# Two heads on the partitions of the sample-token search, whole f32 blocks beside one scatter, and a common budget for two background queues

## The chip, the cores and the metric

The kernel runs on one core of one Trainium2 chip. The metric is the device time of one execution in microseconds (us), lower is better. The profile is one profiled execution of the same program.

## The reference, cut to what matters

One inference step of a two-layer decoder trunk, for 256 prompt tokens and 8 x 8 = 64 sample tokens that share the weights. A layer has a mixing part (retention and a gated recurrence) and then PEER, a retrieval over 128 x 128 single-neuron experts with 8 heads and the 16 best per head:

```
def peer(xn, wq, keys, u_tab, v_tab):
    q = (xf @ wq).reshape(n, PEER_HEADS, 2, PEER_DKEY // 2)
    s = jnp.einsum('nhpd,hpkd->nhpk', q, keys)
    top_s, top_i = lax.top_k(s, PEER_TOPK)
    cand = top_s[:, :, 0, :, None] + top_s[:, :, 1, None, :]
    best_s, best_c = lax.top_k(cand.reshape(n, PEER_HEADS, PEER_TOPK * PEER_TOPK), PEER_TOPK)
    ...
    eidx = (i1 * N_KEYS + i2).reshape(n, PEER_HEADS * PEER_TOPK)
    gate = jax.nn.softmax(best_s, axis=-1)
    ...
        u = jnp.take(u_tab, eb, axis=0)
        hid = jax.nn.gelu(jnp.einsum('nd,nkd->nk', xb, u)) * gb
        v = jnp.take(v_tab, eb, axis=0)
        return jnp.einsum('nk,nkd->nd', hid, v)
```

Each token thus finds the 16 best of 128 keys in each of two halves for each head (the search), the 16 best of their sums (the choice), and takes the weighted rows of 128 experts.

## The kernel before, in words

**Items.** The program is a list of items, one per weight block of 128 x 1024 f32 (512 KB): a layer has 96 blocks of dense weights, the last 16 of them the key projection (wq), and then 256 blocks of the expert tables. `run` walks over the items. For item k it splits block k + 2, issues the load of block k + 5 (`RAWS`) on SP's queue, runs the item's matmuls, and then what was put off to it (`late`, filled by `at`) and the item's `post`. To split (L211) is to make two halves of a block that TensorE can take in one pass: `hi`, a rounded copy by ScalarE (L218), and `lo`, the rest, by VectorE (L220; for most wq blocks by GpSimd). Three matmuls (hi hi, lo hi, hi lo) then stand for one of full width. `hi` and `lo` have three buffers each, the loaded blocks (`raw`) five.

**PEER for the prompt tokens is dense.** All experts are computed for all 256 prompt tokens: phases of 32 blocks each, in the order U1, U0, U3, V1, U2, V0, V3, V2. A U block (`umm`, L917 to L919) has 24 matmuls of 256 columns and makes the hidden values h of 128 experts. A V block (`vmm`, L1125 to L1127) has 12 matmuls of 512 columns; they add h times the block to four accumulators, and h is split too, two blocks ahead (`hsplit`: hh by ScalarE, hl by VectorE, L1108). Between U and V h is multiplied by the gates. Those come by `scatter` (L1038): for each of 32 groups of 8 tokens VectorE builds one-hot tiles sA, sO and sB (L1054 to L1058), TensorE multiplies them (`place`, 16 small matmuls, L1068 and L1069) and VectorE multiplies h with the outcome (L1075); the group g is built in one step, placed in the next and weighed in the one after, so 34 steps in all. The scatter of U1 and U0 runs in U3, that of U3 and U2 in V0.

**Search and choice.** For each of the 16 wq blocks (8 heads, 2 halves) `post_wq` computes the scores one item later and the search one item after that: `top16` (L874), five VectorE operations with three loads of match values, for three token tiles: two of 128 prompt tokens and one of 64 sample tokens. `choose(t)` (L932) makes of them the choice per token tile: a top16 per head over 50 sums, then comparisons and sums over 2048 elements (L966, L974, L978) for the indices. It runs for tile 2 (the sample tokens), 0 and 1.

**The sample tokens are sparse.** `sample` (L1160) gathers for 64 columns one row of the U table per partition (`gather`, an indirect DMA that GpSimd issues, 512 KB, three buffers) and multiplies it with the tokens (L1180), a gather two steps ahead; then the same with the V table (L1192, L1194). The partitions hold the 64 tokens twice, each half with the experts of four heads.

**Two background queues.** `choose` and `scatter` are generators in a queue `bg`, `sample` is one in `bg2`. Twice per item `background` steps them: each queue has a credit, to which half of the item's budget is added, and each step takes off what it yields, a nominal cost in us (a scatter step 2.3, a step of `sample` 1.3). The budgets are written out by phase (`TUNE`, `bg` and `bg2`). At the start of U3 the choosers are drained, at the start of a V phase the scatter that it needs, and three blocks before the end of V2 all that is left.

All engines work off their own instructions in the program's order, so the order in which these generators are stepped is the order on VectorE.

Of the kernel before, what the change touches and what calls it, by code (L numbers as in the profile page):

```python
# [58 lines left out]
def share(i, f):  # L59
    return "pool" if math.floor((i + 1) * f) > math.floor(i * f) else "dve"  # L60


class Background:
# [28 lines left out]
class Trunk:  # L92
# [130 lines left out]
    def run(self):  # L223
        self.items, self.blocks, self.raw, self.hl = [], [], {}, {}
        for l in range(self.depth):
            Layer(self, l).plan()
        self.credit = self.credit2 = 0.0
# [37 lines left out]
class Layer:  # L265
# [5 lines left out]
    def plan(self):  # L271
# [3 lines left out]
        def add(mm, post=None, pre=None, lo="dve", budget=2.0, budget2=0.0):  # L275
            T.items.append(dict(mm=mm, post=post, pre=pre, lo=lo, budget=budget, budget2=budget2))
# [30 lines left out]
        for ph, (kind, q) in enumerate(PHASES):  # L307
            for i in range(PHB):
                e = q * PHB + i
                pre = (lambda kind=kind, q=q: self.phase(kind, q)) if i == 0 else None  # L310
                mm, post = (self.umm, self.post_u) if kind == "U" else (self.vmm, self.post_v2)
                add(mm(q, i), lambda post=post, q=q, i=i: post(q, i), pre=pre, lo=share(i, TUNE["lo"][ph]),
                    budget=TUNE["bg"][ph], budget2=TUNE["bg2"][ph])
                T.blocks.append(a["ut"][e] if kind == "U" else a["peer_v"].rearrange("(p j) d -> j p d", j=KEYS)[e])
# [617 lines left out]
    def choose(self, t):  # L932
        T, nc, pp = self.T, self.nc, self.pp
        n = TOK[t][1]
        m = lambda tag, *x, **k: self.part(("s_" if t == 2 else "p_") + tag, *x, **k)
        vals, idx = self.vals[t], self.idx[t]
        ixh = m("c_ixh", [128, 2 * HEADS, TOPK], F16)
        nc.vector.tensor_copy(ixh[:n], idx[:n].rearrange("p h s k -> p (h s) k"))
        step = m("c_step", [128, 2 * HEADS, TOPK, 2], F16)
        nc.vector.tensor_copy(step[:n, :, 0, :], ixh[:n, :, 0, None].to_broadcast([n, 2 * HEADS, 2]))  # L940
        nc.vector.tensor_tensor(step[:n, :, 1:, :], ixh[:n, :, 1:, None].to_broadcast([n, 2 * HEADS, TOPK - 1, 2]),
                                ixh[:n, :, :TOPK - 1, None].to_broadcast([n, 2 * HEADS, TOPK - 1, 2]), op=OP.subtract)
        yield 0.8
        cand = m("c_cand", [128, HEADS, NCAND])
        off = 0
        for r in range(8):
            w = ROWS[r]
            nc.vector.tensor_tensor(cand[:n, :, off:off + w], vals[:n, :, 0, r:r + 1].to_broadcast([n, HEADS, w]),
                                    vals[:n, :, 1, 0:w], op=OP.add)
            off += w  # L950
        nc.vector.tensor_tensor(cand[:n, :, off:], vals[:n, :, 0, 8:16],
                                vals[:n, :, 1, 0:1].to_broadcast([n, HEADS, 8]), op=OP.add)
        yield 1.2
        best = m("c_best", [128, HEADS, TOPK])
        pos = m("c_pos", [128, HEADS, TOPK], U32)
# [32 lines left out]
        start = m("c_start", [128, HEADS * half, 2], F16)  # L988
# [14 lines left out]
        nc.vector.tensor_tensor(g[:n], g[:n], z[:n, :, None].to_broadcast([n, HEADS, TOPK]), op=OP.mult)  # L1003
# [93 lines left out]

    def hsplit(self, q, i, upto=NPT):
# [11 lines left out]

    def vmm(self, q, i):
        nc, T = self.nc, self.T

        def mm(hi, lo):
            if i + 2 < PHB:
                self.hsplit(q, i + 2)
            else:
                self.look_ahead("V", q, i)
# [146 lines left out]
def prepare(inp, depth):  # L1265
# [11 lines left out]
    for l in range(depth):  # L1277
# [8 lines left out]
        wall[l, 80:96] = fm(i["peer_wq"][l])  # L1286
# [66 lines left out]
```

## Time and profile before

| | |
|---|---|
| median of 3 runs | 2598.59 us (2595.16 to 2600.17) |
| the profiled execution's own time | 2597.29 us |
| its span, first to last instruction | 2595.5 us |
| mean granted TensorE clock | 0.987 |
| TensorE matmul busy | 2429.8 us (94%) |
| VectorE busy | 2060.9 us (79%) |
| ScalarE busy | 1125.4 us (43%) |
| GpSimd busy | 481.1 us (19%) |
| HBM over the span | 203 GB/s |

Busy is the time in which an engine has at least one instruction in work. The durations of instructions that follow one another overlap in the record, on TensorE by much and on VectorE by a little, so a sum of durations is more than the busy time, and the pace is read from the starts. The engine names in the rows are PE (TensorE matmul), PEld (its weight load), DVE (VectorE), ACT (ScalarE), POOL (GpSimd) and SP (the queue that issues the loads). The two layers run alike; windows are given for the first. There the end of wq lies before 471.6 us, and the phases from there are U1 (to 597.8), U0 (to 690.3), U3 (to 817), V1 (to 905.2), U2 (to 997.3), V0 (to 1123), V3 (to 1212.5) and V2 (to 1300).

### The profile page before, as it was taken

The numbers are of one execution on the slowest core, as the hardware profiler recorded it, in microseconds if no ns is written. First come the engines' busy times: TensorE is split into PE (matmuls) and PEld (weight loads), VectorE is DVE, ScalarE is ACT, GpSimd is POOL, SyncE is SP. The second block draws the span as 40 slices with busy tenths as digits, with TensorE's granted clock in tenths as the row PEclk, the third lists the DMA queues.
The fourth block names the chain that finished last, engine by engine and source line by source line (L and its number), as shares of the span: only waits on it lengthen the run. The fifth ranks groups of instructions, "written<-read, shape, count | busy, mean of one in ns | idle before, by whom it ended". The sixth has DMA issues, their size and how long they took to land. (4 is left out here: it accounts for less than half of the span.)

```text
span 2595.5 us, 43089 instructions
## 1 busy us (share of the span) xinstructions
PE 2429.8 (94%) x16636; PEld 2189.7 (84%) x16636; DVE 2060.9 (79%) x3915; ACT 1125.4 (43%) x1687; POOL 481.1 (19%) x305
## 2 busy tenths in 40 slices
PE   8999999889989999899999999998899899998998
PEld 7879888889988898678888799897799888976787
DVE  6465658997799868999874756589978998699997
ACT  4337344344433444344543463443443344433444
POOL 0000004002212421035200000050021233210452
PEclk9999999999999999999999999999999999999999
DMA  6333443347767986579852334343487679865896
GB/s 235 105 110 118 135 152 120 119 162 248 263 200 237 327 292 228 170 262 350 287 192 94 114 122 148 122 145 118 154 278 249 202 257 329 290 204 164 293 353 216
DMA packets 151469, 529.73 MB, mean 204 GB/s; under 512 B 18272, under 2 KB 25440, under 8 KB 150496
## 3 DMA queue, kind: packets, MB, share of 16 engines
q1 hardware_dynamic: 112528, 385.59, 45.2%
q0 software_dynamic: 36864, 134.23, 14.2%
q10 hardware_dynamic: 1872, 7.16, 0.7%
q8 instruction: 130, 2.13, 0.3%
q14 instruction: 75, 0.61, 0.1%
HBM read 520.59 MB, written 6.32 MB: 203 GB/s over the span
## 5 line engine op out<-in xcount | busy, mean ns | idle before, releaser
L220 DVE TENSOR_TENSOR lo<-raw,hi 128x1024 fp32r<-128x1024 f32 x680 | 828.4, 1220 | 315.5 <-ACT hi L218 311.9
L218 ACT CAST hi<-raw 128x1024 fp32r<-128x1024 f32 x704 | 737.5, 1048 | 668.9 <-PE ps_acc L1127 405.6
L919 PE MATMUL ps_h<-xh,lo 128*128 128x256 f32 x2048 | 587.6, 287 | 46.5 <-DVE lo L220 46.4
L917 PE MATMUL ps_h<-xh,hi 128*128 128x256 f32 x2048 | 588.7, 287 | 0.0
L918 PE MATMUL ps_h<-xl,hi 128*128 128x256 f32 x2048 | 582.6, 284 | 0.0
L919 PEld LDWEIGHTS ps_h<-xh,lo 128*128 128x128 f32 x2048 | 396.2, 193 | 55.0 <-DVE lo L220 54.9
L1125 PE MATMUL ps_acc<-hi,hh 128*128 128x512 f32 x1024 | 405.2, 396 | 5.3 <-ACT hh L1107 5.3
L1127 PE MATMUL ps_acc<-hi,hl 128*128 128x512 f32 x1024 | 399.1, 390 | 0.0
L1126 PE MATMUL ps_acc<-lo,hh 128*128 128x512 f32 x1024 | 398.7, 389 | 0.0
L917 PEld LDWEIGHTS ps_h<-xh,hi 128*128 128x128 f32 x2048 | 396.3, 193 | 0.8 <-issue 0.7
L918 PEld LDWEIGHTS ps_h<-xl,hi 128*128 128x128 f32 x2048 | 396.4, 194 | 0.1
L1171 POOL DMA_INDIRECT g<-in_peer_u,eS x128 | 194.8, 1522 | 728.9 <-DVE g L1180 442.8
L349 PE MATMUL ps_acc<-xh,hi 128*128 128x320 f32 x960 | 309.9, 323 | 3.0 <-ACT hi L218 3.0
L351 PE MATMUL ps_acc<-xh,lo 128*128 128x320 f32 x960 | 300.8, 313 | 8.4 <-DVE lo L220 8.4
L350 PE MATMUL ps_acc<-xl,hi 128*128 128x320 f32 x960 | 299.4, 312 | 0.0
L1171 POOL DMA_INDIRECT g<-in_peer_v,eS x128 | 206.8, 1616 | 484.9 <-DVE xs L1194 424.7
L1125 PEld LDWEIGHTS ps_acc<-hi,hh 128*128 128x128 f32 x1024 | 192.3, 188 | 44.8 <-ACT hh L1107 7.0
L1127 PEld LDWEIGHTS ps_acc<-hi,hl 128*128 128x128 f32 x1024 | 192.2, 188 | 40.7
L1126 PEld LDWEIGHTS ps_acc<-lo,hh 128*128 128x128 f32 x1024 | 192.5, 188 | 38.0
L927 ACT ACTIVATE H<-ps_h 128x512 f32<-128x512 f32 x128 | 76.5, 597 | 293.2 <-PE ps_h L919 290.6
L349 PEld LDWEIGHTS ps_acc<-xh,hi 128*128 128x128 f32 x960 | 183.2, 191 | 15.0 <-issue 6.6
L351 PEld LDWEIGHTS ps_acc<-xh,lo 128*128 128x128 f32 x960 | 182.9, 191 | 11.2 <-DVE lo L220 11.0
(277 smaller groups left out, 3480.2 us busy)
## 6 DMA issues: line engine op xcount, KB each, us to landing
raw<-in_ut SPq DMA_DIRECT2D x256, 512.0 KB
raw<-in_peer_v SPq DMA_DIRECT2D x256, 512.0 KB
raw<-in_wall SPq DMA_DIRECT2D x192, 512.0 KB
r<-in_r0t SPq DMA_DIRECT2D x2, 2048.0 KB
out_sr_s<-r ACTq DMA_DIRECT2D x2, 2048.0 KB
aux<-in_c_mP SPq DMA_DIRECT2D x16, 192.0 KB
gw<-in_gates SPq DMA_DIRECT2D x2, 1024.0 KB
H<-in_keyst SPq DMA_DIRECT2D x32, 64.0 KB
```

Source lines behind the costliest of these rows:

```text
L218: nc.scalar.copy(hi, raw)
L220: eng.tensor_tensor(lo, raw, hi.bitcast(F32), op=OP.subtract)
L349: nc.tensor.matmul(o, wh, xh[:, k, :], start=k == 0, stop=False)
L350: nc.tensor.matmul(o, wh, xl[:, k, :], start=False, stop=False)
L351: nc.tensor.matmul(o, wl, xh[:, k, :], start=False, stop=k == 7)
L917: nc.tensor.matmul(o, uh, xh, start=k == 0, stop=False, skip_group_check=True)
L918: nc.tensor.matmul(o, uh, xl, start=False, stop=False, skip_group_check=True)
L919: nc.tensor.matmul(o, ul, xh, start=False, stop=k == 7, skip_group_check=True)
L1125: nc.tensor.matmul(self.acc[t][d], hh[:, s], hi[:, c], start=first, stop=False)
L1126: nc.tensor.matmul(self.acc[t][d], hh[:, s], lo[:, c], start=False, stop=False)
L1127: nc.tensor.matmul(self.acc[t][d], hl[:, s], hi[:, c], start=False, stop=last)
L1171: nc.gpsimd.indirect_dma_start(out=g, out_offset=None, in_=T.a[tab].rearrange("l e d -> (l e) d"), in_offset=bass.IndirectOffsetOnAxis(ap= ...
```

## The change

1. **Search.** The wq blocks are reordered (in the host's layout of the weights, as the two heads are then neighbours) so that heads h and h + 4 follow each other. The queries of the 64 sample tokens of both stand side by side, and their scores fill the two halves of the partitions of one tile, which one top16 searches. Prompt tokens are searched per head as before. The key slots go from 6 to 4, the queries' from 3 of 320 to 2 of 640 columns.
2. **Choice.** `choose(2)` works on 128 partitions and 4 heads in place of 64 and 8; the indices and gates come out as `sample` wants them. The yields of its top16 change from 0.7 to 1.2 (1.25 for the prompt tiles).
3. **Whole blocks.** In V0, the blocks 2, 4, 7, 9, 12, 14, 17, 19, 22, 24, 27 and 29 are not split, nor is their h: four f32 matmuls of 512 columns take both as they are. The load that reuses the slot is issued after these matmuls. The option to make `lo` on GpSimd by share (`share`, all zeros) goes.
4. **One budget.** One credit and one budget per phase: the first queue is stepped, and what it leaves goes to the second.

```
-            bg=(1.9, 1.4, 2.3, 0, 0.1, 2.3, 0.5, 0.1),
-            bg2=(0.1, 0.7, 0.7, 0.9, 0.9, 0.3, 1.1, 0.9),
-            lo=(0, 0, 0, 0, 0, 0, 0, 0))
+            peer=(1.45, 1.6, 2.5, 1.1, 1.66, 2.6, 1.1, 1.2))
...
     def split(self, k):
...
+        if self.items[k]["whole"]:
+            self.hl[k] = (raw, None)
+            return
...
             self.split(k + 2)
-            self.load(k + RAWS)
+            if not it["whole"]:
+                self.load(k + RAWS)
             for _ in it["mm"](*self.hl.pop(k)):
                 self.background(it, 0.5)
+            if it["whole"]:
+                self.load(k + RAWS)
...
     def background(self, it, f):
-        self.credit = min(self.bg.advance(self.credit + f * it["budget"]), 0.0)
-        self.credit2 = min(self.bg2.advance(self.credit2 + f * it["budget2"]), 0.0)
+        left = self.bg2.advance(self.bg.advance(self.credit + f * it["budget"]))
+        self.credit = min(left, 0.0)
...
-    def post_wq(self, c):
+    def post_wq(self, n):
-        h, s = c // 2, c % 2
-        q = self.slot("q", NT, 3)
-        nc.scalar.copy(q, self.p[:, :NT])
-        key = self.slot("key", KEYS, 6)
-        nc.sync.dma_start(key, a["keyst"][:, c, :])
+        h, s, second = n // 4 + n % 2 * 4, n // 2 % 2, n % 2
+        if not second:
+            self.q2 = self.slot("q", 2 * NT, 2)
+        q2 = self.q2
+        if second:
+            nc.scalar.copy(q2[:, NT:NT + NST], self.p[:, NPT:NT])
+            nc.scalar.copy(q2[:, NT + NST:], self.p[:, :NPT])
+            q = q2[:, NT + NST:]
+        else:
+            nc.scalar.copy(q2[:, :NT], self.p[:, :NT])
+            q = q2[:, :NPT]
+        key = self.slot("key", KEYS, 4)
+        nc.sync.dma_start(key, a["keyst"][:, 2 * h + s, :])
...
-            for t, (r0, n) in enumerate(TOK):
-                nc.tensor.matmul(p[:n, t * 128:(t + 1) * 128], q[:, r0:r0 + n], key, start=t == 0, stop=True,
+            for t in range(2):
+                nc.tensor.matmul(p[:, t * 128:(t + 1) * 128], q[:, t * 128:(t + 1) * 128], key, start=t == 0, stop=True,
                                  skip_group_check=True)
+            if second:
+                for t, k in ((2, first_key), (3, key)):
+                    nc.tensor.matmul(p[:, t * 128:(t + 1) * 128], q2[:, NPT:NPT + 2 * NST], k, start=False, stop=True,
+                                     skip_group_check=True)
             nc.scalar.copy(sc[:, 0:2, :], p[:, :256].rearrange("p (t k) -> p t k", t=2))
-            nc.scalar.copy(sc[:64, 2, :], p[:64, 256:384])
+            if second:
+                nc.scalar.copy(sc[:64, 2, :], p[:64, 256:384])
+                nc.scalar.copy(sc[64:, 2, :], p[64:, 384:512])
...
-                for t, (_, n) in enumerate(TOK):
-                    self.top16(self.slot("mr", KEYS, 3)[:n], self.vals[t][:n, h, s, :], self.idx[t][:n, h, s, :], sc[:n, t, :])
+                for t in range(3 if second else 2):
+                    hh = h if t < 2 else h - 4
+                    self.top16(self.slot("mr", KEYS, 3), self.vals[t][:, hh, s, :], self.idx[t][:, hh, s, :], sc[:, t, :])
...
     def choose(self, t):
-        n = TOK[t][1]
+        n, nh = 128, (4 if t == 2 else HEADS)
...
-        for h in range(HEADS):
+        for h in range(nh):
             self.top16(m("c_mr", [128, NCAND], bufs=2)[:n], best[:n, h, :], pos[:n, h, :], cand[:n, h, :])
-            yield 0.7
+            yield 1.2 if t == 2 else 1.25
...
-            for s in range(2):
-                nc.vector.tensor_copy(self.eS[s * 64:(s + 1) * 64], ei[:n, s * 64:(s + 1) * 64])
-                nc.vector.tensor_copy(self.gS[s * 64:(s + 1) * 64], gf[:n, s * 64:(s + 1) * 64])
+            nc.vector.tensor_copy(self.gS, gf)
+            nc.vector.tensor_copy(self.eS, ei)
...
+    def whole(self, kind, q, i):
+        return (kind, q) == ("V", 0) and i > 1 and i % 5 in (2, 4)
+
     def vmm(self, q, i):
+        def direct(w, _):
+            self.hsplit_next(q, i)
+            for t in range(2):
+                for d in range(2):
+                    nc.tensor.matmul(self.acc[t][d], self.h[q][:, i, t * 128:(t + 1) * 128], w[:, d * 512:(d + 1) * 512],
+                                     start=False, stop=False)
+                if t == 0:
+                    yield
+
+        if self.whole("V", q, i):
+            return direct
...
-        wall[l, 80:96] = fm(i["peer_wq"][l])
+        wall[l, 80:96] = fm(i["peer_wq"][l])[[2 * (n // 4 + n % 2 * 4) + n // 2 % 2 for n in range(16)]]
```

`hsplit_next` is the splitting of h two blocks ahead that stood in `mm`, left out where that block is whole. In the rest of `choose` the number of heads, nh, stands in place of `HEADS`.

## Rows read from the trace of the kernel before

**Rows 1.** The page of the profile, its head.
```profile
span 2595.5 us, 43089 instructions
```

**Rows 2.** Stretches: window, length, busy us by engine (instructions), clock, DMA share, GB/s.
```profile
450.00:471.60 21.60, 21.60 (x146) 20.14 (x144) 20.27 (x106) 8.37 (x18) 7.17 (x3) 1.00 0.33 108
471.60:597.80 126.20, 101.65 (x779) 97.10 (x779) 117.65 (x419) 49.20 (x62) 3.06 (x2) 0.97 0.45 145
597.80:690.30 92.50, 92.50 (x774) 92.50 (x773) 64.48 (x81) 44.55 (x54) 24.76 (x18) 1.00 0.83 279
690.30:817.00 126.70, 112.68 (x1281) 108.78 (x1281) 125.02 (x193) 42.31 (x51) 25.28 (x18) 1.00 0.64 206
...
905.20:997.30 92.10, 92.10 (x769) 92.10 (x768) 61.77 (x63) 41.53 (x50) 24.65 (x20) 1.00 0.87 299
997.30:1123.00 125.70, 111.32 (x896) 84.72 (x896) 124.61 (x197) 43.62 (x65) 10.90 (x8) 1.00 0.53 171
1123.00:1212.50 89.50, 87.57 (x394) 72.18 (x390) 82.66 (x96) 43.85 (x66) 47.01 (x27) 1.00 0.93 330
1212.50:1300.00 87.50, 87.22 (x386) 71.93 (x384) 73.78 (x87) 45.50 (x69) 26.82 (x16) 1.00 0.82 293
```

**Rows 3.** VectorE's timeline, searches in the first blocks of U1: start, us.
```profile
472.26 0.28 DVE L876 MAX8 H<-H 128x8 f32<-128x128 f32 x1
...
473.84 0.27 DVE L876 MAX8 H<-H 64x8 f32<-64x128 f32 x1
...
475.38 1.20 DVE L220 TENSOR_TENSOR lo<-raw,hi 128x1024 fp32r<-128x1024 f32 x1
...
492.80 2.33 DVE L220 TENSOR_TENSOR lo<-raw,hi 128x1024 fp32r<-128x1024 f32 x2
```

**Rows 4.** Timeline of VectorE and TensorE, one block of V0.
```profile
1043.19 1.21 DVE L220 TENSOR_TENSOR lo<-raw,hi 128x1024 fp32r<-128x1024 f32 x1
...
1043.33 0.20 PE L1068 MATMUL ps_m<-sB,sA 128*128 128x64 f16 x1 [0.24 <-DVE H L1075]
...
1043.82 0.48 PE L1125 MATMUL ps_acc<-hi,hh 128*128 128x512 f32 x1
...
1044.32 0.42 DVE L1108 TENSOR_TENSOR hl<-H,hh 128x256 fp32r<-128x256 f32 x1
...
1044.65 0.68 DVE L1054 TENSOR_TENSOR sA<-i1T,iota_a 128x1024 f16<-128x1024 f16 x1
...
1046.92 1.21 DVE L220 TENSOR_TENSOR lo<-raw,hi 128x1024 fp32r<-128x1024 f32 x1
```

**Rows 5.** The choice in U1: a group of VectorE's lines, and its timeline.
```profile
L974 DVE TENSOR_TENSOR steps<-H 128x2048 f16<-128x2048 f16 (+1 forms) x8 | 9.7, 1217 | 0.1
...
498.21 0.20 DVE L876 MAX8 H<-H 64x8 f32<-64x50 f32 x1
...
499.36 0.18 DVE L876 MAX8 H<-H 64x8 f32<-64x50 f32 x1
```

**Rows 6.** TensorE by source line (ns min/median/max), and its timeline (start, us).
```profile
L1125 PE MATMUL ps_acc<-hi,hh x1024: 389/389/506, 817.0 to 2585.7; 128*128 128x512 f32 x171
...
L721 PEld LDWEIGHTS ps_m<-xc,gw x64: 187/190/338, 191.4 to 1509.2; 128*128 128x128 f32 x64
L721 PE MATMUL ps_m<-xc,gw x64: 452/452/939, 191.4 to 1509.5; 128*128 128x344 f32 x64
...
200.22 1.32 PE L721 MATMUL ps_m<-xc,gw 128*128 128x344 f32 x4
```

**Rows 7.** DMA issues by line: count, median us to landing; in U0, V0, V3.
```profile
g<-in_peer_u,eS POOLq DMA_INDIRECT x18, 6.4
...
g<-in_peer_v,eS POOLq DMA_INDIRECT x8, 5.2
...
g<-in_peer_v,eS POOLq DMA_INDIRECT x27, 7.6
```

**Rows 8.** A stretch of 30 us in V3, columns as in rows 2.
```profile
1180.00:1210.00 30.00, 30.00 (x134) 24.83 (x133) 27.17 (x32) 14.96 (x23) 16.41 (x10) 1.00 0.98 362
```

More of the change, by code (lines that the diff above doesn't have):

```diff
@@ L226, in run @@
             Layer(self, l).plan()
-        self.credit = self.credit2 = 0.0
+        self.credit = 0.0
         for k, it in enumerate(self.items):
@@ L273, in plan, with add @@
         n0 = len(T.items)
-        def add(mm, post=None, pre=None, lo="dve", budget=2.0, budget2=0.0):
-            T.items.append(dict(mm=mm, post=post, pre=pre, lo=lo, budget=budget, budget2=budget2))
+        def add(mm, post=None, pre=None, lo="dve", budget=2.0, whole=False):
+            T.items.append(dict(mm=mm, post=post, pre=pre, lo=lo, budget=budget, whole=whole))
         x = lambda: (T.xh, T.xl)
@@ L311, in plan @@
                 mm, post = (self.umm, self.post_u) if kind == "U" else (self.vmm, self.post_v2)
-                add(mm(q, i), lambda post=post, q=q, i=i: post(q, i), pre=pre, lo=share(i, TUNE["lo"][ph]),
-                    budget=TUNE["bg"][ph], budget2=TUNE["bg2"][ph])
+                add(mm(q, i), lambda post=post, q=q, i=i: post(q, i), pre=pre, budget=TUNE["peer"][ph],
+                    whole=self.whole(kind, q, i))
                 T.blocks.append(a["ut"][e] if kind == "U" else a["peer_v"].rearrange("(p j) d -> j p d", j=KEYS)[e])
@@ L849, in part @@
         return v
-    def post_wq(self, c):
+    def post_wq(self, n):
         T, nc, a = self.T, self.nc, self.a
-        h, s = c // 2, c % 2
-        q = self.slot("q", NT, 3)
-        nc.scalar.copy(q, self.p[:, :NT])
-        key = self.slot("key", KEYS, 6)
-        nc.sync.dma_start(key, a["keyst"][:, c, :])
+        h, s, second = n // 4 + n % 2 * 4, n // 2 % 2, n % 2
[11 more added lines that the diff above has]
+        nc.sync.dma_start(key, a["keyst"][:, 2 * h + s, :])
+        if not second:
+            self.key = key
+        first_key = self.key
         def scores():
@@ L933, in choose @@
         T, nc, pp = self.T, self.nc, self.pp
-        n = TOK[t][1]
+        n, nh = 128, (4 if t == 2 else HEADS)
         m = lambda tag, *x, **k: self.part(("s_" if t == 2 else "p_") + tag, *x, **k)
-        vals, idx = self.vals[t], self.idx[t]
-        ixh = m("c_ixh", [128, 2 * HEADS, TOPK], F16)
+        vals, idx = self.vals[t][:, :nh], self.idx[t][:, :nh]
+        ixh = m("c_ixh", [128, 2 * nh, TOPK], F16)
         nc.vector.tensor_copy(ixh[:n], idx[:n].rearrange("p h s k -> p (h s) k"))
[L939 to L942, printed above, removed]
+        step = m("c_step", [128, 2 * nh, TOPK, 2], F16)
+        nc.vector.tensor_copy(step[:n, :, 0, :], ixh[:n, :, 0, None].to_broadcast([n, 2 * nh, 2]))
+        nc.vector.tensor_tensor(step[:n, :, 1:, :], ixh[:n, :, 1:, None].to_broadcast([n, 2 * nh, TOPK - 1, 2]),
+                                ixh[:n, :, :TOPK - 1, None].to_broadcast([n, 2 * nh, TOPK - 1, 2]), op=OP.subtract)
         yield 0.8
-        cand = m("c_cand", [128, HEADS, NCAND])
+        cand = m("c_cand", [128, nh, NCAND])
         off = 0
@@ L951, in choose @@
         nc.vector.tensor_tensor(cand[:n, :, off:], vals[:n, :, 0, 8:16],
[L952 removed]
+                                vals[:n, :, 1, 0:1].to_broadcast([n, nh, 8]), op=OP.add)
         yield 1.2
[L954 to L956 removed]
+        best = m("c_best", [128, nh, TOPK])
+        pos = m("c_pos", [128, nh, TOPK], U32)
@@ L957, in choose @@
+        for h in range(nh):
             self.top16(m("c_mr", [128, NCAND], bufs=2)[:n], best[:n, h, :], pos[:n, h, :], cand[:n, h, :])
-            yield 0.7
+            yield 1.2 if t == 2 else 1.25
         half = TOPK // 2
-        place = m("c_place", [128, HEADS, half, 2], F16)
+        place = m("c_place", [128, nh, half, 2], F16)
         nc.vector.tensor_copy(place[:n].rearrange("p h a b -> p h (a b)"), pos[:n])
-        found = [m(f"c_f{i}", [128, HEADS * TOPK], bufs=2) for i in range(2)]
+        found = [m(f"c_f{i}", [128, nh * TOPK], bufs=2) for i in range(2)]
@@ L964, in reached @@
         def reached(at, marks):
-            v = m("c_row", [128, HEADS, half, TOPK, 2], F16)
+            v = m("c_row", [128, nh, half, TOPK, 2], F16)
             nc.vector.tensor_tensor(v[:n].rearrange("p h a k b -> p (h a) k b"),
-                                    at[:n].rearrange("p h a b -> p (h a) b")[:, :, None, :].to_broadcast([n, HEADS * half, TOPK, 2]),
-                                    self.marks[:n, marks][:, None].to_broadcast([n, HEADS * half, TOPK, 2]), op=OP.is_ge)
+                                    at[:n].rearrange("p h a b -> p (h a) b")[:, :, None, :].to_broadcast([n, nh * half, TOPK, 2]),
+                                    self.marks[:n, marks][:, None].to_broadcast([n, nh * half, TOPK, 2]), op=OP.is_ge)
@@ L969, in reached @@
             return v
         def summed(out, v, steps):
-            w = pp.tile([128, HEADS, half, TOPK, 2], F16, tag="g4", name="steps", bufs=3)
+            w = pp.tile([128, nh, half, TOPK, 2], F16, tag="g4", name="steps", bufs=3)
             run = lambda x: x.rearrange("p h a k b -> p h a (k b)")
-            nc.vector.tensor_tensor(run(w)[:n], run(v)[:n], steps.to_broadcast([n, HEADS, half, 2 * TOPK]), op=OP.mult)
+            nc.vector.tensor_tensor(run(w)[:n], run(v)[:n], steps.to_broadcast([n, nh, half, 2 * TOPK]), op=OP.mult)
@@ L987, in choose @@
         yield 2.6
-        start = m("c_start", [128, HEADS * half, 2], F16)
+        start = m("c_start", [128, nh * half, 2], F16)
         summed(start[:n], row, self.marks[:n, 1].rearrange("p k b -> p (k b)")[:, None, None])
@@ L996, in choose @@
         yield 2.6
-        g = m("c_g", [128, HEADS, TOPK], bufs=2)
-        z = m("c_z", [128, HEADS])
-        nc.vector.tensor_tensor(g[:n], best[:n], best[:n, :, 0:1].to_broadcast([n, HEADS, TOPK]), op=OP.subtract)
+        g = m("c_g", [128, nh, TOPK], bufs=2)
+        z = m("c_z", [128, nh])
+        nc.vector.tensor_tensor(g[:n], best[:n], best[:n, :, 0:1].to_broadcast([n, nh, TOPK]), op=OP.subtract)
         nc.scalar.activation(g[:n], g[:n], AF.Exp)
@@ L1096, in look_ahead, with hsplit_next @@
             self.hsplit(q, i - PHB + 2, self.weighed[q // 2] // half * half)
+    def hsplit_next(self, q, i):
+        if i + 2 >= PHB:
+            self.look_ahead("V", q, i)
+        elif not self.whole("V", q, i + 2):
+            self.hsplit(q, i + 2)
     def hsplit(self, q, i, upto=NPT):
@@ L1109, in hsplit @@
             self.hid[q, i][2] = upto
+    def whole(self, kind, q, i):
+        return (kind, q) == ("V", 0) and i > 1 and i % 5 in (2, 4)
     def vmm(self, q, i):
         nc, T = self.nc, self.T
+        def direct(w, _):
[8 more added lines that the diff above has]
+            return direct
         def mm(hi, lo):
[L1115 to L1118, printed above, removed]
+            self.hsplit_next(q, i)
             hh, hl, _ = self.hid.pop((q, i))
```

12 lines of the change are left out of this document (5 added, 7 removed).

## The prediction

> **What bounds the kernel now.** The profiled execution took 2597.29 us by its own time, of which the span is 2595.5 [rows 1]; the 1.8 us around it stay. The median of the three runs shown is 2598.59, 1.3 above it. I looked first at the busy time of the engines phase by phase. In U0, U2 and V2 TensorE is busy in practically the whole stretch [rows 2]: 32 blocks take 92.1 us in U2 and 87.5 in V2, 2.88 and 2.73 us a block. That is TensorE's own pace, and in these phases no other engine sets the end. U1, U3 and V0 have the same 32 blocks each and take 126.2, 126.7 and 125.7 us; there VectorE is busy for 117.65, 125.02 and 124.61 us, and TensorE is not [rows 2]. So 34, 35 and 38 us a layer, some 214 us in the two layers, are VectorE's: this is what can be won. V3, at 89.5, loses two more, to a scatter step that is drained before its first block.
>
> Why VectorE is late in U1 begins before it. At the end of the key projection (wq) it is busy for 20.27 of 21.6 us [rows 2]. One top16 takes it 1.58 us over 128 partitions and 1.54 over 64 [rows 3]: it costs the same with half of the partitions empty. Three per block are 4.7 us, VectorE falls behind, and the last search ends at 492.8 [rows 3], 21 us into U1.
>
> **The change part by part.**
>
> *Search.* A layer has 16 x 2 + 8 = 40 top16 in place of 48: 12.5 us less of VectorE. Two wq blocks then cost it 7.8 us where they cost 9.4, so it catches up before U1, and what is left in U1 are the five searches of the last two blocks, 8 us, where twelve, 18 us, lay there. TensorE's scores remain six small matmuls a pair; ScalarE gets one copy more a pair and is busy for 8.37 of 21.6 us [rows 2]. Nothing is charged for these; without the cover a copy would cost its own duration, under half a us, 16 times. The key tiles turn over in four slots, not six; each is read up to two blocks after its load is issued, which hides it. Uncovered, a pair of scores would wait 0.2 us (64 KB at the rate of [rows 8]) and the issue.
>
> *Choice of the sample tokens.* Four heads in place of eight, on 128 partitions. Four top16 less, 1.15 us each (499.36 - 498.21) [rows 5], are 4.6 us; the five widest operations (products and comparisons of 2048 f16, 1.22 us [rows 5]) are halved, some 3 us, and their additions give about as much: 10 us in all. By the new budgets, counting the yields, only two of the three choosers run in U1, and choose(1) moves whole into U0. That takes about 17 us out of U1 (eight top16, the two first sums and what is ahead of them; its end lay in U0 already). VectorE in U1: 117.65 - 10 - 10 - 17 = 81 us, below the 92.1 that TensorE needs. U1 should fall to TensorE's pace with the scores of the last wq blocks, 94 us: -32. U0 has room for the chooser: its VectorE is busy for 64.48 of 92.5 us [rows 2], a third of that with gathered rows that now come later.
>
> *One budget.* The sample generator now runs only where the first queue is empty. Counting yields before gives 17, 17, 20, 8, 27 and 17 products of gathered rows in U0, U3, U2, V0, V3 and V2; POOL issued 18, 18, 20, 8, 27 and 16 gathers there [rows 2], so the count can be trusted. After, I count 17, 2, 38, 5, 27 and 12 (and 27 in V1). U3 has 33 scatter steps and two products. One scatter step takes VectorE 2.27 us, the split of a block 1.13, hl 0.33 (differences of the starts [rows 4]). U3 is then 32 x 1.13 + 33 x 2.27 + 2.4 = 113.5 us, and no scatter step is left to be drained ahead of V1: -13.
>
> *Whole blocks in V0.* One block has 12 matmuls of 512 columns in 2.73 us, 0.227 us each, while one is recorded with 389 ns [rows 6]: 0.162 us of a record lies beside the next one. A 4-byte matmul that is not split is recorded twice (the gate projection: 64 records for 32 calls), and four such passes of 344 columns take 1.32 us [rows 6]; less 0.16 that is 0.29 a pass, so 0.43 at 512 columns. A whole block has eight such passes, 3.44 us against 2.73: +0.71 of TensorE, while VectorE is spared 1.13 + 0.33. Placing one scatter step takes TensorE 0.49 us (1043.33 to 1043.82 [rows 4]). V0 then needs of TensorE 20 x 2.73 + 12 x 3.44 + 33 x 0.49 = 112 us, of VectorE 20 x 1.46 + 33 x 2.27 + 5 x 1.2 = 110. Both engines work in order and are nearly even, so neither runs quite free; I take 115: -10.7. The bounds are 112, full overlap, and 121, if half of the 96 weight loads of 0.19 us [rows 6] show between the passes. V3 no longer begins with a drained step: -2.2. The load behind a whole block is issued after its matmuls, and SP keeps the later loads behind it; they are needed three blocks, 10 us, later, and V0 moves only 171 GB/s [rows 2], so this costs nothing; uncovered, a block would wait some 1.4 us for it (0.524 MB at the 362 GB/s of [rows 8]).
>
> *Where the gathers go.* This speaks against the change. A gather fills one of three buffers, and POOL issues the next when the product has been taken, so three gathers turn round in no less than latency + 0.3 (product to issue) + 1.2 (product). From issue to landing it is 5.2 us in V0, at 171 GB/s, 6.4 in U0, at 279, and 7.6 in V3, at 330 [rows 2, 7]. U2 now wants 38 products in 92.1 us, one every 2.31; with the weight blocks that is 70 x 0.524 = 36.7 MB, near 400 GB/s. The most I find over 30 us is 362 GB/s, at a DMA share of 0.98 [rows 8]. At 7.0 us, between the rows, a gather comes every 2.83 us: 38 take 108, and U2 becomes 109 us, since VectorE waits in order, the split behind it is late and TensorE waits for that: +17 (0 at 5.4 us of latency, +23 at 7.6). The last 16 blocks of U0 want one every 2.35 us; 17 x 0.48 = 8, less 4 that the two blocks split ahead give as slack: +4. V1 and V3 want one every 3.3 us, which V3 did before: nothing.
>
> The Trainium skill speaks against these 17 us. Its page "DMA: Bandwidth & Descriptors", Anatomy of one DMA, SWDGE path, puts a DMA at 2.0 us plus its bytes at 436 GB/s, an estimate of 3.2 us here; with 1.7 of POOL the buffers would yield a gather every 2.1 us, and U2 would stay at 92. Its page "HBM Reference", Specifications, gives a core that streams alone about 425 GB/s, by which U2's bytes take 86 us. V3's 7.6 us and the 362 GB/s agree with neither [rows 7, 8].
>
> **Sum per layer:** -32 - 13 - 10.7 - 2.2 + 4 + 17 = -36.9; two layers -73.8; 2597.3 - 73.8 = 2523.5, and I say 2524.
>
> **The rivals.**
>
> *The gathers stay hidden*, with a latency of 5.4 us or less in U2 and U0. For it: 5.2 in V0 [rows 7]. Against: 7.6 at 330 GB/s, and U2 would have to move 400. It would give -57.9 a layer, 2597.3 - 116 = 2482. The rule of the Trainium skill's page on DMA, above, comes to this.
>
> *Weight loads of whole blocks are exposed.* All eight passes take 0.19 us more, 4.95 us a block; V0 needs 20 x 2.73 + 12 x 4.95 + 16 = 130 us, +4 in place of -10.7: 2554. For it: no row shows 512 columns of this form. Against: the four passes of 344 columns leave no room for a load between them [rows 6].
>
> *The search backlog stays*, because the first wq blocks carry other VectorE work: U1 at 104 us, 2544.
>
> *Slower than before:* the three gather buffers become the bound in every phase. All gains are 57.9 us a layer; at 3.28 us a gather U2 loses 37, U0 16 and V1, V2 and V3 some 5 together, and the gain is gone. It decides from 8.3 us of latency on, in all phases. For it: latency rises with the load [rows 7]. Against: 7.6 is the median of the fullest phase.
>
> *It doesn't do what it says:* the halves share partitions but VectorE's time stays. [Rows 3] exclude it, since time there doesn't go with partitions.
>
> **How the numbers follow.** Forecast (U2 held by the gathers, V0 between 112 and 121): 0.53, its own range 2505 to 2545. Gathers hidden 0.22, weight loads 0.09, backlog 0.09, slower 0.05, all else 0.02. The range 2480 to 2557 takes in the first four. The runs before lie 0.2% apart, about what can be told from no change: faster 0.93, same 0.02, slower 0.05.
>
> **What would show it.** Right: U1 near 94 us with no wq search later than 12 us into it, U3 near 114, V0 near 115 with whole blocks of 3.4 us plus scatter, and in U2 products that wait for DMA and lie 2.8 us apart. Wrong: U2 at 92 us (then 2482), V0 above 121 with TensorE alone busy, or U1 above 100 with splits as what TensorE waits for.

## The result, and the profile after

The changed kernel takes 2559.91 us, the median of 4 runs (2555.3 to 2570.66), beside 2599.38 for the kernel before, the median of 4: a ratio of 0.9855, 95% interval 0.9819 to 0.9892. The forecast was 2524, with a range from 2480 to 2557, so the direction was right, and just over half of the gain forecast is there. The profiled execution took 2555.3 us, 42.0 less than that of before; the fence shows the head of its page (the span) and, from the chain of work that ended last, the shares of the span by line.

```profile
span 2553.4 us, 42587 instructions
...
DMA g<-in_peer_v,eS 5%; POOL g L1206 4%; PE ps_acc L349 2%; PE ps_acc L351 2%; PE ps_acc L350 2%; PE ps_h L937 2%; PE ps_h L935 2%; PE ps_h L936 2%; DVE lo L217 1%; DVE xs L1229 1%; PE ps_acc L1161 1%; PE ps_acc L1162 1%; PE ps_acc L1160 1%
```

The gathered rows (g) and the GpSimd instruction that issues their gathers (L1206; 1206 is the changed file's line) now carry 9% of the chain. The same stretches as in [rows 2], the end of wq and then U1, U0, U3, V1, U2, V0, V3 and V2, with the same columns:

```profile
439.70:461.30 21.60, 21.60 (x157) 21.60 (x157) 18.65 (x89) 9.90 (x23) 8.22 (x4) 1.00 0.47 142
461.30:557.70 96.40, 93.69 (x780) 93.31 (x779) 83.54 (x261) 46.35 (x57) 0.00 (x0) 1.00 0.55 175
557.70:656.10 98.40, 95.03 (x776) 94.43 (x776) 79.82 (x169) 47.98 (x60) 27.67 (x18) 0.98 0.74 255
656.10:775.90 119.80, 113.02 (x1283) 110.46 (x1282) 110.98 (x166) 41.91 (x50) 2.61 (x2) 0.99 0.49 161
775.90:864.10 88.20, 88.13 (x387) 71.89 (x386) 79.36 (x120) 43.33 (x63) 45.87 (x28) 1.00 0.93 338
864.10:977.40 113.30, 98.98 (x770) 97.13 (x769) 81.85 (x90) 41.58 (x50) 56.99 (x38) 0.95 0.90 321
977.40:1097.80 120.40, 116.55 (x851) 77.89 (x850) 109.09 (x176) 27.56 (x41) 6.35 (x5) 0.99 0.52 170
1097.80:1184.80 87.00, 87.00 (x385) 72.09 (x384) 77.74 (x89) 43.46 (x64) 46.99 (x26) 1.00 0.96 346
1184.80:1276.70 91.90, 89.27 (x385) 71.34 (x383) 71.41 (x84) 45.42 (x68) 21.07 (x12) 1.00 0.74 258
```

The reader is to see three things. U1 lost 30 us and stands near TensorE's pace: busy for 93.69 of 96.4 us. U2 grew from 92.1 to 113.3 and issues 38 gathers, as counted. And three phases for which no wait for gathers was forecast are longer than forecast: U3 119.8 (114 forecast), V0 120.4 (115), V2 91.9 (87.5). Here each phase's change, as the mean of the two layers, stands beside its forecast (a phase is read from its first matmul to the next phase's; wq from the starts of its last blocks):

| us per layer | U1 | U0 | U3 | V1 | U2 | V0 | V3 | V2 | wq |
|---|---|---|---|---|---|---|---|---|---|
| forecast | -32 | +4 | -13 | 0 | +17 | -10.7 | -2.2 | 0 | 0 |
| measured | -29.1 | +5.3 | -6.6 | +0.1 | +18.3 | -5.1 | -1.1 | +3.9 | -4.6 |

The sums are -36.9 and -18.8 a layer. The two layers' 37.6 leaves 4.4 of the 42.0 us. They lie in the main ahead of wq in the first layer, where no part of the change runs: wq begins at 393.05 us where it began at 398.12 (the last section tells of such differences).

What TensorE waits for, first in U2, then in the first 14 us of U3 and the longest wait in the first 13 of V0 (total us, times, longest):

```profile
PE ps_h L937 <- DVE lo L217: 14.3, 9, 3.9
```

```profile
PE ps_m L1085 <- DVE sB L1075: 3.0, 1, 3.0
```

```profile
PE ps_m L1085 <- DVE sB L1075: 3.3, 1, 3.3
```

In U2 it waits for the split (`lo`), and the split waits in VectorE's order behind products of gathered rows that haven't landed; VectorE's own waits there:

```profile
DVE xs L1229 <- DMA g<-in_peer_v,eS: 14.2, 9, 3.4
DVE g L1215 <- DMA g<-in_peer_u,eS: 14.0, 13, 2.3
```

U3 and V0 begin with one wait for the scatter's first tile. VectorE's timeline across the border from U2 to V0 (977.4) shows where it is from:

```profile
979.95 1.28 DVE L1229 SCALAR_TENSOR_TENSOR xs<-g,cS,xs 128x1024 f32<-128x1024 f32 x1 [1.46 <-DMA g<-in_peer_v,eS]
981.15 1.22 DVE L217 TENSOR_TENSOR lo<-raw,hi 128x1024 fp32r<-128x1024 f32 x1
982.28 0.42 DVE L1131 TENSOR_TENSOR hl<-H,hh 128x256 fp32r<-128x256 f32 x1
982.62 0.69 DVE L1071 TENSOR_TENSOR sA<-i1T,iota_a 128x1024 f16<-128x1024 f16 x1
```

A product that belongs to U2's items waits 1.46 us for its rows and starts at 979.95, 2.5 us into V0. The split, hl and the scatter's first tiles stand behind it. V0 itself has hardly a gather, but it inherits what U2 left. U3 inherits the end of U0 in the same way: the last product of U0 starts at 658.01, 1.9 us into U3, after a wait of 1.73 for its rows.

### The profile page after: what moved, and what is told of

Same layout as the page of the kernel before. It is cut to its first block, busy times and chain, and to the rows that moved or that the text cites. A ratio compares the mean times of both kernels' runs of the same rounds, so it can differ in the third digit from the quotient of the medians.

```text
span 2553.4 us, 42587 instructions
## 1 busy us (share of the span) xinstructions
PE 2429.0 (95%) x16540; PEld 2174.7 (85%) x16540; DVE 1981.8 (78%) x3663; ACT 1096.6 (43%) x1647; POOL 493.8 (19%) x305
## 5 line engine op out<-in xcount | busy, mean ns | idle before, releaser
L215 ACT CAST hi<-raw 128x1024 fp32r<-128x1024 f32 x680 | 712.5, 1048 | 702.2 <-PE ps_acc L1162 362.5
L217 DVE TENSOR_TENSOR lo<-raw,hi 128x1024 fp32r<-128x1024 f32 x656 | 799.3, 1221 | 240.6 <-ACT hi L215 234.6
L937 PE MATMUL ps_h<-xh,lo 128*128 128x256 f32 x2048 | 588.6, 287 | 36.9 <-DVE lo L217 36.8
L1160 PE MATMUL ps_acc<-hi,hh 128*128 128x512 f32 x928 | 371.1, 400 | 0.0
L1161 PE MATMUL ps_acc<-lo,hh 128*128 128x512 f32 x928 | 363.9, 392 | 7.1 <-DVE lo L217 6.9
L1162 PE MATMUL ps_acc<-hi,hl 128*128 128x512 f32 x928 | 364.5, 393 | 1.0 <-DVE hl L1131 1.0
L1206 POOL DMA_INDIRECT g<-in_peer_u,eS x128 | 198.4, 1550 | 714.1 <-DVE g L1215 424.6
L1206 POOL DMA_INDIRECT g<-in_peer_v,eS x128 | 216.4, 1691 | 399.6 <-DVE xs L1229 361.5
L1161 PEld LDWEIGHTS ps_acc<-lo,hh 128*128 128x128 f32 x928 | 175.0, 189 | 49.9 <-DVE lo L217 12.8
L1162 PEld LDWEIGHTS ps_acc<-hi,hl 128*128 128x128 f32 x928 | 174.7, 188 | 41.3 <-DVE hl L1131 2.1
L1215 DVE SCALAR_TENSOR_TENSOR g<-g,xs 128x1024 f32<-128x1024 f32 x128 | 156.6, 1223 | 64.7 <-DMA g<-in_peer_u,eS 64.4
L1160 PEld LDWEIGHTS ps_acc<-hi,hh 128*128 128x128 f32 x928 | 175.0, 189 | 36.6 <-issue 2.9
L1229 DVE SCALAR_TENSOR_TENSOR xs<-g,cS,xs 128x1024 f32<-128x1024 f32 x126 | 161.8, 1284 | 55.6 <-DMA g<-in_peer_v,eS 54.8
```

What stands on the lines that cost most here:

```text
L937: nc.tensor.matmul(o, ul, xh, start=False, stop=k == 7, skip_group_check=True)
L1160: nc.tensor.matmul(self.acc[t][d], hh[:, s], hi[:, c], start=first, stop=False)
L1161: nc.tensor.matmul(self.acc[t][d], hh[:, s], lo[:, c], start=False, stop=False)
L1162: nc.tensor.matmul(self.acc[t][d], hl[:, s], hi[:, c], start=False, stop=last)
L1206: nc.gpsimd.indirect_dma_start(out=g, out_offset=None, in_=T.a[tab].rearrange("l e d -> (l e) d"), in_offset=bass.IndirectOffsetOnAxis(ap= ...
```

## The experiments

Theory A: the gathers come at the pace of their three buffers, and all the time that is missing against the sum without gathers is theirs, borders and V2 included. Rivals: the new budgets ask more of VectorE and TensorE than the phases have, whatever the gathers do (B); the bytes of gathers and weights together are too many (C); or the whole blocks cost more than forecast. The first layer's phases in each run (us):

| | U1 | U0 | U3 | V1 | U2 | V0 | V3 | V2 | median, us |
|---|---|---|---|---|---|---|---|---|---|
| before | 126.2 | 92.5 | 126.7 | 88.2 | 92.1 | 125.7 | 89.4 | 87.2 | 2599.4 |
| after | 96.3 | 98.4 | 119.8 | 88.2 | 113.3 | 120.4 | 87.0 | 91.8 | 2559.9 |
| no gathers | 96.3 | 92.8 | 115.4 | 87.1 | 92.1 | 115.1 | 87.0 | 87.2 | 2482.5 |
| spread | 97.0 | 92.8 | 115.7 | 87.4 | 92.1 | 115.2 | 89.9 | 94.4 | 2504.7 |
| no whole blocks | 96.3 | 96.5 | 121.9 | 89.3 | 111.0 | 127.9 | 89.0 | 92.3 | 2579.9 |
| two budgets | 98.8 | 96.9 | 126.8 | 88.2 | 92.1 | 114.5 | 87.2 | 87.2 | 2521.7 |
| four loads ahead | 96.3 | 98.1 | 120.8 | 87.2 | 108.8 | 120.7 | 87.0 | 93.8 | 2563.6 |
| ring of four | 96.3 | 92.8 | 117.2 | 87.1 | 92.2 | 117.4 | 87.0 | 87.2 | 2492.1 |
| search and choice alone | 100.3 | 96.9 | 126.8 | 88.2 | 92.1 | 125.8 | 91.0 | 87.2 | 2544.1 |
| ring of four, spread | 97.0 | 92.9 | 115.7 | 87.1 | 92.1 | 114.6 | 87.0 | 87.2 | 2482.2 |

**No gathers.** The kernel leaves out the gathers: the products, those of the V table too, read a resident tile.

```
-            nc.gpsimd.indirect_dma_start(out=g, ...)
...
-                nc.vector.scalar_tensor_tensor(g, g, 1.0, self.xs, ...)
+                nc.vector.scalar_tensor_tensor(g, T.x[0], 1.0, self.xs, ...)
...
```

> After, without the gathers: the products read a tile that is there, so the sample tokens' outputs are not those of the reference; VectorE's work and the order of all else stay. Theory A (products wait for the three gather buffers, and the lag is carried into U3 and V0): U0 92.5, U2 92 us, U3 114, V0 114 to 115, V2 87; 2475 to 2485 us in all. Theory B (the new budgets ask more of VectorE and TensorE than the phases have, whatever the gathers do): U2 and U0 stay over 100 and 97 us, 2540 to 2555.

It took 2482.51 us, ratio 0.9533 (0.951 to 0.9556). Its windows of U2, V0 and V2:

```profile
864.20:956.30 92.10, 92.10 (x769) 92.10 (x768) 82.17 (x92) 41.66 (x50) 0.00 (x0) 1.00 0.57 183
956.30:1071.40 115.10, 114.86 (x851) 76.88 (x850) 106.50 (x173) 27.56 (x41) 0.00 (x0) 1.00 0.45 147
1158.40:1245.60 87.20, 87.20 (x385) 71.91 (x383) 67.79 (x80) 45.44 (x68) 0.00 (x0) 1.00 0.60 188
```

VectorE does the same work there as after (82.17 us against 81.85 in U2), and all of U2's 21 us, V0's 5 and V2's 4.7 are gone. What was missing comes with the gathers (their issue, latency or transfer), and not from the budgets' work: B, which expected 2540 us or more, is out. V0 is the 115 of the forecast, so the whole blocks were priced rightly.

**Spread.** The same 128 gathers a layer, with the budget's steps laid evenly over the phases.

```
-            peer=(1.45, 1.6, 2.5, 1.1, 1.66, 2.6, 1.1, 1.2))
+            peer=(1.75, 1.25, 2.5, 1.12, 1.22, 2.6, 1.12, 1.2))
```

> After, with budgets 1.75, 1.25, 2.5, 1.12, 1.22, 2.6, 1.12, 1.2: the same gathers, but one every 3.0 us or more in every phase in which they run. Theory A: under the cap of three buffers at 7 us of latency, so U0 93, U2 93 to 95, U3 114, V0 115, V1, V2 and V3 88 to 90; 2480 to 2500 us. Theory C (it is the bytes: DMA moves no more than about 360 GB/s): V1, V2 and V3 now want 365 GB/s and grow as U2 shrinks; 2515 to 2535. Theory B: half of the gain, about 2530.

It took 2504.66 us, ratio 0.9637 (0.961 to 0.9665): 55 less than after, but 5 above theory A's range, and V2 came at 94.4 where 88 to 90 was expected. U2, V3 and V2:

```profile
855.80:948.00 92.20, 92.20 (x770) 92.19 (x769) 71.33 (x84) 41.73 (x50) 44.92 (x28) 1.00 0.95 345
1063.20:1153.10 89.90, 88.03 (x385) 71.81 (x384) 80.95 (x92) 43.44 (x64) 49.64 (x28) 1.00 0.95 343
1153.10:1247.50 94.40, 90.30 (x385) 71.27 (x383) 82.80 (x94) 45.53 (x68) 39.57 (x23) 1.00 0.88 315
```

U2 with 28 gathers in place of 38 doesn't hold TensorE up. V3 and V2 do, with 28 and 23: at 2.73 us a block V3 would last 87 us, so that its 28 gathers want one every 3.1, and V2's 23 are all issued in its first 72 us, one every 3.2. The three buffers are near their limit at that.

**No whole blocks.** `whole` always answers no.

```
-        return (kind, q) == ("V", 0) and i > 1 and i % 5 in (2, 4)
+        return False
```

> After, with every block of V0 split as before. My sum: V0 is then VectorE's, 32 x 1.46 + 33 x 2.27 + 5 x 1.2, 122 to 126 us in place of 115 and what the gathers add ahead of it: 2570 to 2580 us. Rival (TensorE's 0.71 us a block takes back what VectorE saves): 2552 to 2560.

It took 2579.85 us, ratio 0.9928 (0.9899 to 0.9956): 20 more than after, and V0 is back at 127.9 (122 to 126 expected).

```profile
976.10:1104.00 127.90, 111.70 (x898) 85.86 (x897) 124.08 (x198) 43.84 (x65) 4.86 (x4) 0.99 0.47 152
```

VectorE is busy for 124.08 of it, as in [rows 2]. The whole blocks do gain: 20 us here, 22 beside the old budgets (below), where -10.7 and -2.2 a layer, 26 in all, were forecast. By the lengths of V0 and V3 in the profiles it is 19 here and 30 there.

**Two budgets.** The change with the two old budgets, `bg` and `bg2` (their values are those that the change takes out).

```
-        left = self.bg2.advance(self.bg.advance(self.credit + f * it["budget"]))
-        self.credit = min(left, 0.0)
+        self.credit = min(self.bg.advance(self.credit + f * it["budget"]), 0.0)
+        self.credit2 = min(self.bg2.advance(self.credit2 + f * it["budget2"]), 0.0)
```

> After, with the two budgets of before (search, choice and whole blocks stay). Theory A: gathers as spread as before, none waits for long; U1 96 to 100 us, U0 and U2 92.5, U3 126 (17 products beside the scatter), V0 116, V3 89: 2510 to 2520 us, faster than after. Rival (the one budget is what wins in U1, by moving a chooser to U0): U1 at 115, 2550 or more.

It took 2521.71 us, ratio 0.9685 (0.9661 to 0.9708): without the one budget the rest of the change is 38 us faster than the whole of it. U3 and U2:

```profile
667.90:794.70 126.80, 112.74 (x1282) 108.85 (x1281) 125.11 (x193) 42.33 (x51) 25.35 (x18) 1.00 0.63 207
882.90:975.10 92.20, 92.20 (x770) 92.17 (x769) 61.89 (x63) 41.53 (x50) 24.71 (x20) 1.00 0.87 299
```

U3 keeps its 18 gathers and is VectorE's again; U2 with 20 is free. U0 was expected at 92.5 and took 96.9: TensorE waits there twice for a split that stands behind steps of the choice, 2.2 us in all, and no product waits for its rows.

**Search and choice alone.** The same without whole blocks.

> Search and choice over two heads alone: two budgets as before the change and no block that stays whole. If the blocks that stay whole are worth the same beside the old budgets as beside the new ones (some 20 us in all): 2540 to 2548 us, with V0 at 124 to 126. Rival (what they are worth comes from the single budget): about 2525 us, with V0 near 115.

It took 2544.08 us, ratio 0.9772 (0.9739 to 0.9806). V0 is at 125.8; the two budgets' run, which has the whole blocks, took 22 us less (2521.71), so what they win doesn't come from the one budget. The first expectation holds, the rival doesn't.

**Four loads ahead**, the control for the next run: `RAWS` 4 in place of 5.

> The kernel after with four staging buffers for the weight loads instead of five, which frees 4 KB of each partition; the control for the run with a fourth gather buffer. Both theories: 2550 to 2575 us, as the kernel after; U2 near 113, V0 near 120. If four loads ahead are too few, the time goes up by waits of the split's instructions for weights.

It took 2563.59 us, ratio 0.985 (0.9809 to 0.989), as after. Its U2:

```profile
871.60:980.40 108.80, 97.00 (x770) 95.54 (x769) 81.08 (x90) 41.63 (x50) 56.16 (x37) 0.97 0.89 332
```

**Ring of four.** The same with a fourth gather buffer, which takes the room that the fifth load had.

```
-            g = pp.tile([128, D], F32, tag="g4", name="g4", bufs=3)
+            g = pp.tile([128, D], F32, tag="g4", name="g4", bufs=4)
```

> The kernel after with four staging buffers and four buffers for the gathered rows instead of three. Theory A (the gathers come at the pace of the three buffers: about 7 us of latency and 1.5 us of product and issue in one turn of the ring, 8.5/3 = 2.8 us for one gather where the budget wants one in 2.3): with four buffers 8.5/4 = 2.1 us, so U2 at 92 to 97 us, U0 at 93, U3 and V0 at 115, and 2485 to 2510 us in all. Theory C (the gathers and the weight loads are too many bytes for the time): U2 stays at 105 us or more, and the time at 2540 or more.

It took 2492.12 us, ratio 0.958 (0.9546 to 0.9614): 71 us less than its control for one buffer. U3 and V0 came at 117, where 115 was expected. U0, U2, V0 and V2:

```profile
556.60:649.40 92.80, 92.80 (x776) 92.80 (x775) 79.96 (x170) 47.98 (x60) 29.47 (x20) 1.00 0.77 274
...
853.70:945.90 92.20, 92.20 (x769) 92.16 (x769) 80.47 (x89) 41.74 (x50) 53.82 (x37) 1.00 0.99 379
945.90:1063.30 117.40, 115.19 (x851) 76.81 (x850) 108.80 (x176) 27.66 (x41) 6.70 (x6) 1.00 0.52 178
...
1150.30:1237.50 87.20, 87.20 (x385) 71.91 (x383) 67.79 (x80) 45.45 (x68) 16.18 (x10) 1.00 0.75 256
```

U2 moves the same bytes in 92.2 us, at 379 GB/s, where the kernel after moved 321 and was held up. Rival C is out. What is left in V0 is its first block: products of U2's last items, the last at 946.88, still stand ahead of the scatter, which begins at 949.54, and TensorE waits 1.7 us for it. VectorE's products in U2, first of the kernel after, with GpSimd's gather for the last of them ahead:

```profile
905.97 1.68 POOL L1206 DMA_INDIRECT g<-in_peer_u,eS  x1 [0.60 <-DVE g L1215]
```

```profile
904.48 1.22 DVE L1215 SCALAR_TENSOR_TENSOR g<-g,xs 128x1024 f32<-128x1024 f32 x1
...
909.14 1.23 DVE L1215 SCALAR_TENSOR_TENSOR g<-g,xs 128x1024 f32<-128x1024 f32 x1 [2.31 <-DMA g<-in_peer_u,eS]
...
911.94 1.23 DVE L1215 SCALAR_TENSOR_TENSOR g<-g,xs 128x1024 f32<-128x1024 f32 x1 [1.56 <-DMA g<-in_peer_u,eS]
...
914.47 1.22 DVE L1215 SCALAR_TENSOR_TENSOR g<-g,xs 128x1024 f32<-128x1024 f32 x1 [0.16 <-DMA g<-in_peer_u,eS]
```

and then of the ring of four:

```profile
888.10 1.68 POOL L1206 DMA_INDIRECT g<-in_peer_u,eS  x1 [0.60 <-DVE g L1215]
```

```profile
886.60 1.22 DVE L1215 SCALAR_TENSOR_TENSOR g<-g,xs 128x1024 f32<-128x1024 f32 x1
...
888.88 1.22 DVE L1215 SCALAR_TENSOR_TENSOR g<-g,xs 128x1024 f32<-128x1024 f32 x1
...
890.25 1.23 DVE L1215 SCALAR_TENSOR_TENSOR g<-g,xs 128x1024 f32<-128x1024 f32 x1
...
892.76 1.23 DVE L1215 SCALAR_TENSOR_TENSOR g<-g,xs 128x1024 f32<-128x1024 f32 x1
...
896.66 1.23 DVE L1215 SCALAR_TENSOR_TENSOR g<-g,xs 128x1024 f32<-128x1024 f32 x1 [1.52 <-DMA g<-in_peer_u,eS]
```

In the turn shown a gather is issued 0.27 us after the product that empties its buffer (904.48 + 1.22 = 905.70, and 905.97), and the product that it feeds starts 8.5 us later, in both kernels. One turn of the ring is 10.0 us in the one (904.48 to 914.47) and 10.1 in the other (886.60 to 896.66). Three products fit in it in the one, four in the other. The turn shown of the kernel after is a long one. Over U2 of the first layer, by the starts of gathers and products in the two timelines, the products that waited for their rows start 7.7 us after the gather's issue in the kernel after (the median of 21; the shortest 5.9) and 7.9 us in the ring of four (of 12). With 0.27 and 1.22 that makes a turn of 9.2 us in the kernel after, a gather every 3.06 over three buffers where 2.98 was measured (113.3/38), and one every 2.35 over four, less than the 2.43 that U2 wants (92.2/38): there the ring no longer sets the pace.

**Ring of four, spread.** Both together.

> The budgets spread evenly over the phases, four staging buffers and four buffers for the gathered rows. Theory A: the waits for gathers that V3 and V2 still have with three buffers (about 9 us in each layer) go away: 2485 to 2497 us. Theory C: about 2505 us, as with three buffers. Above 2505 us: four loads ahead are too few.

It took 2482.24 us, ratio 0.9545 (0.9509 to 0.9581), within 0.3 us of the median of the run that gathers nothing (2482.51) and below the range that theory A gave. VectorE's products by line, with its idle time ahead of them in us at the end of each row:

```profile
L1229 DVE SCALAR_TENSOR_TENSOR xs<-g,cS,xs 128x1024 f32<-128x1024 f32 x126 | 161.2, 1279 | 0.1
L1215 DVE SCALAR_TENSOR_TENSOR g<-g,xs 128x1024 f32<-128x1024 f32 x128 | 156.1, 1219 | 0.0
```

In the kernel after the same groups have 55.6 and 64.7 us of idle time. Here V0 has TensorE busy for all of its 114.6 us. This version is faster than the kernel before by 4.5%, and than the kernel after by about 3% (2482.24 against 2559.91, beside runs of before whose medians agree to 0.06%).

## Why the prediction was wrong

**The search:** right in size in U1 (96.3 and 97.8 us against 94), though eight searches and not five still lie there, the last ends 14.6 us in (the prediction's sign was 12), and one block waits 2.7 us for the split behind them. It was undersold ahead of U1. "Nothing is charged for these" was wrong for wq, where TensorE's own scores got shorter: a block took 4.52 us and takes 4.41 and 3.97 in turn, 4.19 on average, so that 14 blocks give 4.6 us a layer. A pair of blocks has six matmuls for the scores in both kernels, as the prediction says, each recorded twice; but in the kernel before two of the six have weights of only 64 columns, the queries of one head's sample tokens. The weight loads of 14 blocks, with TensorE's idle time ahead of them in us at the end of each row, before and then after:

```profile
L349 PEld LDWEIGHTS ps_acc<-xh,hi 128*128 128x128 f32 x112 | 21.0, 187 | 2.4 <-issue 2.4
L863 PEld LDWEIGHTS ps_m<-H 128*64 128x64 f32 x28 | 2.7, 134 | 1.7
```

```profile
L349 PEld LDWEIGHTS ps_acc<-xh,hi 128*128 128x128 f32 x111 | 20.9, 188 | 0.0
L878 PEld LDWEIGHTS ps_m<-H 128*128 128x128 f32 x28 | 3.7, 192 | 0.0
```

In the kernel before TensorE paused in each block for 0.12 us before the 64 columns and 0.17 us after them, 4.1 of the 4.6 us, and the profile names no engine that it waited for. With two heads in 128 columns both pauses are gone. No run changes this shape alone, so it is argued from these rows, and not shown, that the shape makes the pauses.

**The choice:** right; VectorE is busy for 83.5 us in U1 where 81 was worked out.

**One budget:** the count was right (18, 2, 38, 5 and 12 gathers issued in U0, U3, U2, V0 and V2, where 17, 2, 38, 5 and 12 products were counted). U3's -13 came as -6.6: 115.4 in the run without gathers against 113.7 forecast, and the other 4.8 us come with the gathers; in the first layer 3.0 of them are the wait at its start, for the lag that U0 hands over.

**Whole blocks:** right, in V0's length and in a block's. V0 is 115.1 without gathers. In the ring of four with spread budgets the eight passes of a whole block start at 1054.04, the second matmul after them at 1057.70, and one matmul takes 0.23, so a block takes 3.43 us (3.44 forecast).

**The gathers: the step that failed.** The sum had 4 us for U0, 17 for U2 and nothing elsewhere, +21 a layer. Against the run without gathers they cost 42.3 us in the first layer (U0 to V2) and 38.0 in the second. U0 and U2 alone were near: +5.3 for 4, and +18.3 for 17, a gather every 2.98 us in the first layer (113.3/38) and 2.83 in the second (107.7/38), where 2.83 was forecast. That fit is partly luck: the 7.0 us of latency were chosen between rows, while the gathers of U2 itself took 7.6 in the kernel before, at 299 GB/s, by which the sum has +23, and the two layers lost 21 and 16. Two things were left out. U3 and V0 were summed as if VectorE came to them on time, but U0 and U2 want gathers to their very end, and the products that are late there cost the next phase about 5 us. And V2 has no term in the sum, and no reason is given: its 12 gathers are few for 32 blocks. But all 12 are issued between 1185.06 and 1218.29, in its first 34 us, one every 3.0, as dense as in U2, and cost 3 to 5 us. The count of the missing time: U3 6.4, V0 5.6, V2 3.9, U0, U2 and V3 3.8 and U1 2.9 a layer, less 4.6 for wq, is 18.1 a layer or 36.2 in all; 4.4 came back outside these stretches. 2523.5 + 36.2 - 4.4 is 2555.3, the profiled execution's time. That the median lies only 3 us above the range is in part luck: wq's 9 us in the two layers, which the forecast did not have, offset as much of the gathers' price.

**The rivals:** "the gathers stay hidden" gave 2482 us, and that is what the run without gathers and the last one show. The ring's arithmetic by which I took 2.83 us was right, and so the rule of the Trainium skill ("DMA: Bandwidth & Descriptors", Anatomy of one DMA, SWDGE path; an estimate of 3.2 us for a gather) isn't borne out: of the 7.7 us from issue to the waiting product in U2 GpSimd's issue is mostly 1.68, and 6.0 is left, 4.2 in the shortest case. "V0 above 121", "the backlog stays" and the slower case don't hold. The slower case was summed wrongly besides: 38 gathers at 3.28 us are 124.6, so U2 would lose 33 us, not 37, and some of the gain would be left.

## What to carry to other kernels

Where a ring of buffers feeds an engine that works in order, count the turn (latency, product, issue) over the number of buffers against the demand of the busiest stretch, before moving work into it: one buffer more, or the same gathers laid evenly, was worth more here (71 and 55 us) than the whole change (39). When a stall is forecast in a phase, add what the phase after it has to make up, unless that engine has room there. And judge a change of several parts one part at a time: here one part, on a ring of three, lost 38 us of the 78 that the others had won. What the two old budgets would take with a ring of four no run shows.

## What the runs showed that was not expected

With four buffers U2 moved 379 GB/s over 92 us, at a DMA share of 0.99, above the 362 that I took for the most [rows 8]. The latency grew little with that load: the products that wait start 7.7 us after the gather's issue at 321 GB/s with three buffers and 7.9 at 379 with four in the first layer, 6.9 and 8.2 in the second (medians, the second layer's of 25 and 11). With four buffers only the slower gathers are waited for, so the pairs can't be compared closely, and whether load or this choice makes the difference stays open.

TensorE's clock fell after some of its waits. In U2 of the kernel after TensorE waited 1.73 us for a split, went on at 901.4, and from 902.2 ran at the lower of its two levels (1.2 GHz) for 3.4 us, fully busy; the granted clock (third from the end) before and in that stretch:

```profile
900.00:902.20 2.20, 0.82 (x7) 0.82 (x8) 1.34 (x4) 0.38 (x1) 1.68 (x1) 1.00 0.87 339
902.20:905.60 3.40, 3.40 (x19) 3.40 (x18) 3.40 (x4) 0.00 (x0) 1.68 (x1) 0.50 0.88 287
```

Such a stretch follows three of the nine waits in U2. Over all of U2 the clock is 0.95, in the ring of four, without those waits, 1.00. TensorE is busy for 98.98 us of U2, 6.8 more than there, and idle for the other 14.3; whether U2 would be shorter at the full clock no run shows. And executions of kernels that are alike there differ by some 10 us ahead of U1, in the dense weights: of the nine profiles of the kernel after and the experiments, U1 of the first layer starts at 460.3 to 463.5 us in six and at 469.1 to 472.6 in three. Between 150 and 170 us the kernel with two budgets, which starts U1 at 472.3, and then the kernel after, at 461.3:

```profile
150.00:170.00 20.00, 20.00 (x78) 17.03 (x77) 9.64 (x30) 2.80 (x5) 0.00 (x0) 0.55 0.17 53
```

```profile
150.00:170.00 20.00, 19.47 (x122) 16.62 (x123) 14.56 (x46) 4.23 (x8) 0.00 (x0) 1.00 0.24 79
```

At a clock of 0.55 TensorE is busy throughout and does 78 matmuls where the other does 122. Nothing of the change runs there; what decides which of the two an execution gets stays open. For comparisons of a few us the phases' lengths served better than the medians.
